# Column sums of a 268 MB matrix on one core: half-precision casting loads and matmuls replaced by float32 loads, a fold on VectorE and matmuls in four column groups

## The chip, the cores and the metric

The kernel runs on one core of a Trainium2 chip. The metric is device time in microseconds (us), from the runs of the kernel; the median of three runs stands for it. A profile of one execution shows when each engine worked; its times count from the start of the span, which goes from the first to the last instruction.

## The reference

The input is float32, 32 x 1024 x 2048. It is summed over its first two axes, so that 32,768 rows become one row of 2,048 sums:

```python
def reference(grad_output):            # (32, 1024, 2048), float32
    return np.sum(grad_output, axis=(0, 1)).astype(np.float32)   # (2048,)
```

Every byte of the input, 268.44 MB, has to be read from HBM once; the output has 8 KB.

## The kernel before

The rows are cut into blocks of 128 rows, one row per partition (1 MB of float32). A plan, made in Python ahead of the instructions, lists the loads in order. Each entry has its first row, the number m of rows per partition, the type in SBUF, the issuing engine and the columns.

- Two entries with m = 1 stay float32 and are issued by the sync engine (SP), as the first loads of the kernel.
- Thirty entries with m = 8 (8 MB in HBM, each partition reading 64 KB in one piece) are issued by GpSimd (POOL), whose DMA queue casts float32 to float16 on the way, so that half the bytes arrive in SBUF. A smaller leftover entry, with m = 2, and a taper of m = 4 and m = 2 follow, then five with m = 1, and the last 128 rows come as four loads of 512 columns each.
- An entry with m > 1 is halved by one VectorE addition in float16 (L152), into a tile `c`. Three buffers are kept for the big `t` tiles and three for `c`.
- TensorE sums over the partitions: a matmul (L161) with a column of ones as the weights turns 128 x 512 values into 1 x 512, added up in PSUM. There are four such accumulators, `psum0` to `psum3`, one for each 512 columns, and each is a single row. In half precision a tile with m = 8 costs 16 matmuls.
- At the end ScalarE and VectorE copy the four accumulators to `res` in turn (L175, L177), and SP sends the 8 KB out (L178).

The tile framework puts in the waits. Each engine works through its instructions in the order of the program, and each of the engines that issue loads does so too. A load into a reused buffer waits until the readers of its old contents are done. The loads themselves share the core's 16 DMA engines.

Of the kernel before, what the change touches and what calls it, by code (L numbers as in the profile page):

```python
# [1 line left out]

# [4 lines left out]

P = 128
MM_N = 512  # L10

PRE_TILES = 2
PRE_M = 1
PRE_ENGS = ("sync", "sync")
BULK_M = 8
BULK_TAPER = (4, 2)
USE_DVE = True
TAIL_TILES = 5
COL_SPLIT_LAST = True
T_BUFS = 3  # L20
C_BUFS = 3
TAIL_BUFS = 8
BULK_ENGS = ("gpsimd",)
OUT_COPY_ENGS = ("scalar", "vector")


@with_exitstack
def kernel(
    ctx: ExitStack,
    tc: tile.TileContext,  # L30
    grad_output: bass.AP,
    out: bass.AP,
):
    nc = tc.nc
    fp32 = mybir.dt.float32
    fp16 = mybir.dt.float16

    D = out.shape[-1]
    flat = grad_output.rearrange("b s d -> (b s) d")
    R = flat.shape[0]  # L40
    assert R % P == 0 and D % MM_N == 0
    nbanks = D // MM_N
    n_row_blocks = R // P

    pre_tiles = min(PRE_TILES, n_row_blocks // PRE_M // 4)
    col_split = COL_SPLIT_LAST and nbanks > 1
    taper = [m for m in BULK_TAPER if m < BULK_M]
    n_small = TAIL_TILES + (1 if col_split else 0)
    while pre_tiles * PRE_M + sum(taper) + n_small > n_row_blocks:
        if TAIL_TILES and n_small > 1:  # L50
            n_small -= 1
        elif taper:
            taper = taper[1:]
        else:
            col_split = False
            n_small = min(n_small, 1)
            break
    n_tail = n_small - (1 if col_split else 0)

    plan: list = []  # L60
    row = 0
    for i in range(pre_tiles):
        plan.append((row, PRE_M, fp32, PRE_ENGS[i % len(PRE_ENGS)], 0, D))
        row += P * PRE_M
    tail_start = R - P * (n_small + sum(taper))
    bi = 0
    while row < tail_start:
        take = min(P * BULK_M, tail_start - row)
        plan.append((row, take // P, fp16, BULK_ENGS[bi % len(BULK_ENGS)], 0, D))
        bi += 1  # L70
        row += take
    for m in taper:
        plan.append((row, m, fp16, BULK_ENGS[bi % len(BULK_ENGS)], 0, D))
        bi += 1
        row += P * m
    for _ in range(n_tail):
        plan.append((row, 1, fp16, BULK_ENGS[bi % len(BULK_ENGS)], 0, D))
        bi += 1
        row += P
    if col_split:  # L80
        for b in range(nbanks - 1, -1, -1):
            plan.append((row, 1, fp16, BULK_ENGS[bi % len(BULK_ENGS)], b * MM_N, MM_N))
            bi += 1
        row += P
    assert row == R

    io_pool = ctx.enter_context(tc.tile_pool(name="io", bufs=T_BUFS))
    pre_pool = None
    if pre_tiles:
        pre_pool = ctx.enter_context(tc.tile_pool(name="pre", bufs=pre_tiles))  # L90
    c_pool = None
    if USE_DVE:
        c_pool = ctx.enter_context(tc.tile_pool(name="csum", bufs=C_BUFS))
    n_small_tiles = n_tail + (nbanks if col_split else 0)
    tail_pool = None
    if n_small_tiles:
        tail_pool = ctx.enter_context(
            tc.tile_pool(name="tail", bufs=min(n_small_tiles, TAIL_BUFS))
        )
    const_pool = ctx.enter_context(tc.tile_pool(name="const", bufs=1))  # L100
    psum_pool = ctx.enter_context(tc.tile_pool(name="psum", bufs=1, space=bass.MemoryType.PSUM))

    ones16 = const_pool.tile([P, 1], fp16)
    nc.vector.memset(ones16[:], 1.0)  # L104
    ones32 = None
    if pre_tiles:
        ones32 = const_pool.tile([P, 1], fp32)
        nc.vector.memset(ones32[:], 1.0)  # L108

    accs = [  # L110
        psum_pool.tile([1, MM_N], fp32, tag=f"psum{b}", name=f"psum{b}")
        for b in range(nbanks)
    ]
    res = const_pool.tile([1, D], fp32)

    def uses_dve(entry) -> bool:
        _, m, dt_, _, _, col_n = entry
        return USE_DVE and dt_ is fp16 and m > 1 and col_n == D

    def n_chunks(entry) -> int:  # L120
        _, m, dt_, _, _, col_n = entry
        n = (m * col_n) // MM_N
        return n // 2 if uses_dve(entry) else n

    total_mm = [0] * nbanks
    for e in plan:
        for j in range(n_chunks(e)):
            total_mm[((e[4] + j * MM_N) % D) // MM_N] += 1
    started = [False] * nbanks
    n_mm = [0] * nbanks  # L130

    for i, entry in enumerate(plan):
        row0, m, dt_, eng_name, col_lo, col_n = entry
        rows = flat[row0 : row0 + m * P]
        if col_n == D:
            src = rows.rearrange("(p m) d -> p (m d)", p=P)
        else:
            src = rows[:, col_lo : col_lo + col_n]

        if dt_ is fp16:  # L140
            big = m > 1 and col_n == D
            pool, tag = (io_pool, "T") if big else (tail_pool, "Ttail")
            T = pool.tile([P, m * col_n], fp16, tag=tag, name=f"t{i}")
        else:
            T = pre_pool.tile([P, m * col_n], fp32, tag="Tpre", name=f"t{i}")
        getattr(nc, eng_name).dma_start(out=T[:], in_=src)  # L146

        red = T
        if uses_dve(entry):
            half = (m * col_n) // 2  # L150
            C = c_pool.tile([P, half], fp16, tag="C", name=f"c{i}")
            nc.vector.tensor_tensor(  # L152
                out=C[:], in0=T[:, :half], in1=T[:, half:], op=mybir.AluOpType.add
            )
            red = C

        w = ones16 if dt_ is fp16 else ones32
        for j in range(n_chunks(entry)):
            b = ((col_lo + j * MM_N) % D) // MM_N
            n_mm[b] += 1  # L160
            nc.tensor.matmul(  # L161
                accs[b][:, :],
                lhsT=w[:],
                rhs=red[:, j * MM_N : (j + 1) * MM_N],
                start=(not started[b]),
                stop=(n_mm[b] == total_mm[b]),
            )
            started[b] = True

    bank_order = list(range(nbanks - 1, -1, -1)) if col_split else list(range(nbanks))  # L170
    for k, b in enumerate(bank_order):
        eng = OUT_COPY_ENGS[k % len(OUT_COPY_ENGS)]
        dst = res[:, b * MM_N : (b + 1) * MM_N]
        if eng == "scalar":
            nc.scalar.copy(out=dst, in_=accs[b][:, :])  # L175
        else:
            nc.vector.tensor_copy(out=dst, in_=accs[b][:, :])  # L177
    nc.sync.dma_start(out=out[None, :], in_=res[:])  # L178


# [1 line left out]
_INS = ['grad_output']  # L182
_OUTS = [((2048,), 'float32')]


# [23 lines left out]
```

## Time and profile before

| what | value |
|---|---|
| three runs, median (lowest to highest) | 628.81 us (628.43 to 628.89) |
| span of the profiled execution, the only time that the page has of it | 627.2 us |
| HBM read over the span | 268.44 MB, 428 GB/s |
| share of 16 DMA engines, GpSimd's casting queue | 98.9% |
| busy: TensorE matmuls / VectorE / GpSimd | 31% / 22% / 4% |
| mean granted TensorE clock | 0.650 of full speed |

The page counts the bytes that were written to SBUF (135 MB for the most part in float16), so its GB/s of DMA is about half of what was read from HBM. The median of the runs is 1.6 us over the profiled span; what lies outside the span is not seen in the profile.

### The profile page before, as it was taken

The page shows a single profiled execution, that of the slowest core. Times are in us where ns is not written, and L with a number is a line of the kernel's source. Part 1 is how long each engine was busy: PE and PEld are TensorE (multiplying, and loading weights), DVE is VectorE, ACT ScalarE, POOL GpSimd, SP SyncE. Part 2 cuts the span into 40 slices and gives each one's busy share as a digit, 9 for nine tenths or more (in the row PEclk, how much of TensorE's full clock was granted, in tenths as well). Part 3 has the DMA queues.
Part 4 walks back from the last instruction along what each step waited for, and adds up shares of the span by engine and source line. Part 5 has one row for each costly group of instructions (what it writes and reads, how often), then busy time and mean ns, then how long its engine had stood idle before and what let it go on. Part 6 is the DMA issues. An engine that isn't in the chain of part 4 may idle for free.

```text
span 627.2 us, 1267 instructions
## 1 busy us (share of the span) xinstructions
PE 195.1 (31%) x536; PEld 58.1 (9%) x536; DVE 138.9 (22%) x37; ACT 2.4 (0%) x3; POOL 22.6 (4%) x46
## 2 busy tenths in 40 slices
PE   3323320333203333123341134321333312343165
PEld 0001100011000111001110011100111000111011
DVE  0202222022220122211222202222022221122320
ACT  0000000000000000000000000000000000000000
POOL 1000000000000000000000000000000000000110
PEclk9677556775567665667655776656676567665677
DMA  9999999999999999999999999999999999999997
GB/s 242 226 234 201 234 201 234 202 232 203 232 203 232 203 232 203 232 204 230 205 230 205 230 205 230 205 230 206 228 207 228 207 224 211 224 211 221 206 206 139
DMA packets 6344, 135.36 MB, mean 216 GB/s; under 512 B 705, under 2 KB 1217, under 8 KB 1857
## 3 DMA queue, kind: packets, MB, share of 16 engines
q0 software_dynamic: 6048, 133.17, 98.9%
q1 hardware_dynamic: 290, 2.11, 0.9%
q8 instruction: 4, 0.07, 0.0%
q14 instruction: 2, 0.02, 0.0%
HBM read 268.44 MB, written 0.01 MB: 428 GB/s over the span
## 4 chain that ended last, share of the span: by engine, by line
another core or an unknown queue 66%; DVE 21%; DMA 11%; PE 1%; POOL 1%; issue 0%; DVEq 0%; POOLq 0%
DVE c L152 20%; DMA t<-in_grad_output_dram 11%; PE psum L161 1%; POOL t L146 1%; DVEq L152 0%; DVE res L177 0%; POOLq L193 0%
## 5 line engine op out<-in xcount | busy, mean ns | idle before, releaser
L161 PE MATMUL psum<-c,ones 128*1 128x512 f16 x496 | 175.9, 533 | 405.5 <-DVE c L152 405.5
L152 DVE TENSOR_TENSOR c<-t 128x8192 f16<-128x8192 f16 (+2 forms) x33 | 137.5, 4167 | 471.1 <-DMA t<-in_grad_output_dram 471.1
L161 PEld LDWEIGHTS <-ones 128*1 128x1 f16 x520 | 56.5, 109 | 537.5 <-issue 516.4
L146 POOL DMA_DIRECT2D t<-in_grad_output_dram x42 | 22.4, 538 | 590.4 <-DVE c L152 575.3
L161 PE MATMUL psum<-t,ones 128*1 128x512 f16 (+1 forms) x40 | 19.4, 639 | 23.5 <-DMA t<-in_grad_output_dram 23.5
L177 DVE COPY res<-psum 1x512 f32<-1x512 f32 x2 | 1.4, 679 | 13.9 <-PE psum L161 13.9
L161 PEld LDWEIGHTS psum<-t,ones 128*1 128x1 f32 x16 | 1.6, 106 | 27.5 <-DMA t<-in_grad_output_dram 14.1
L175 ACT COPY res<-psum 1x512 f32<-1x512 f32 x2 | 1.1, 575 | 621.1 <-PE psum L161 621.1
L175 ACT ACT_TABLE_LOAD x1 | 1.3, 1283 | 0.7 <-PEq L193 0.7
L104 DVE MEMSET ones<- 128x1 f16 x1 | 0.1, 59 | 0.8 <-PEq L193 0.8
L193 POOL MEMSET const-float32-0.0<- 128x1 f32 x1 | 0.1, 100 | 0.2 <-issue 0.2
L193 POOL MEMSET const-bfloat16-1.0<- 128x1 bf16 x1 | 0.1, 103 | 0.0
L193 POOL MEMSET const-float32-1.0<- 128x1 f32 x1 | 0.1, 100 | 0.0
L193 POOL MEMSET const-uint8-127<- 128x1 uint8 x1 | 0.1, 100 | 0.0
L108 DVE MEMSET ones<- 128x1 f32 x1 | 0.1, 59 | 0.0
## 6 DMA issues: line engine op xcount, KB each, us to landing
t<-in_grad_output_dram POOLq DMA_DIRECT2D x30, 4096.0 KB, 53.1
t<-in_grad_output_dram POOLq DMA_DIRECT2D x5, 512.0 KB, 20.4
t<-in_grad_output_dram SPq DMA_DIRECT2D x2, 1024.0 KB, 14.3
t<-in_grad_output_dram POOLq DMA_DIRECT2D x2, 1024.0 KB, 26.6
t<-in_grad_output_dram POOLq DMA_DIRECT2D x1, 2048.0 KB, 29.0
t<-in_grad_output_dram POOLq DMA_DIRECT2D x4, 128.0 KB, 16.1
out_dram<-res SPq DMA_DIRECT2D x1, 8.0 KB
```

The costliest lines, as they stand in the source:

```text
L104: nc.vector.memset(ones16[:], 1.0)
L108: nc.vector.memset(ones32[:], 1.0)
L146: getattr(nc, eng_name).dma_start(out=T[:], in_=src)
L152: nc.vector.tensor_tensor(out=C[:], in0=T[:, :half], in1=T[:, half:], op=mybir.AluOpType.add)
L161: nc.tensor.matmul(accs[b][:, :], lhsT=w[:], rhs=red[:, j * MM_N : (j + 1) * MM_N], start=(not started[b]), stop=(n_mm[b] == total_mm[b]),)
L175: nc.scalar.copy(out=dst, in_=accs[b][:, :])
L177: nc.vector.tensor_copy(out=dst, in_=accs[b][:, :])
L193: nc = _bacc.Bacc("TRN2", target_bir_lowering=False, num_devices=1)
```

## The change

All loads become float32, issued by SP. There are 32 tiles of 1,024 rows. The first 31 are loaded whole (8 MB, 64 KB in each partition) into one of three buffers; in place, three VectorE additions fold the eight rows in each partition to four, two and one; then TensorE sums that one row over the partitions. The last tile's eight rows per partition are not folded: 128 rows each are loaded by themselves, the last of them in two pieces (1,536 and 512 columns), and each goes straight to TensorE.

The sums are laid out anew. The 2,048 columns are cut into a left part of 1,536 and a right part of 512, and each part into four groups, of 384 and of 128 columns. Group g has weights of 32 columns of ones at the array's columns 32g to 32g + 31, and writes PSUM partitions 32g to 32g + 31, all 32 of them the same sum. One row of a tile so takes four matmuls of 384 columns into `accl` and four of 128 columns into `accr`. At the end ScalarE copies `accl` and issues the store of the left part, VectorE copies `accr` and SP issues the store of the right.

```diff
-PRE_TILES = 2
-BULK_M = 8
-BULK_TAPER = (4, 2)
-TAIL_TILES = 5
-BULK_ENGS = ("gpsimd",)
+ROWS = 8
+RING = 3
+GROUPS = 4
+RIGHT = 512
...
-        getattr(nc, eng_name).dma_start(out=T[:], in_=src)
-            nc.vector.tensor_tensor(
-                out=C[:], in0=T[:, :half], in1=T[:, half:], op=mybir.AluOpType.add
-            )
-            nc.tensor.matmul(
-                accs[b][:, :],
-                lhsT=w[:],
-                rhs=red[:, j * MM_N : (j + 1) * MM_N],
...
+    def add_left(row):
+        seen["l"] += 1
+        for g in range(GROUPS):
+            nc.tensor.matmul(
+                accl[g * G : (g + 1) * G, :lw],
+                lhsT=ones[:],                       # 128 x 32, float32
+                rhs=row[:, g * lw : (g + 1) * lw],  # lw = 384
+                start=seen["l"] == 1,
+                stop=seen["l"] == n_rows,
+                tile_position=(0, g * G),
+            )
+
+    def add_right(row):                             # the same, accr, rw = 128
...
+    for i in range(n_tiles - 1):
+        T = io.tile([P, ROWS * D], fp32, tag="T", name=f"t{i}")
+        src = flat[i * P * ROWS : (i + 1) * P * ROWS].rearrange(
+            "(p m) d -> p (m d)", p=P
+        )
+        nc.sync.dma_start(out=T[:], in_=src)
+        m = ROWS // 2
+        while m >= 1:
+            nc.vector.tensor_tensor(
+                out=T[:, : m * D],
+                in0=T[:, : m * D],
+                in1=T[:, m * D : 2 * m * D],
+                op=mybir.AluOpType.add,
+            )
+            m //= 2
+        add_left(T[:, :D])
+        add_right(T[:, :D])
+
+    T = io.tile([P, ROWS * D], fp32, tag="T", name="tail")
+    base = (n_tiles - 1) * P * ROWS
+    for r in range(ROWS):
+        src = flat[base + r * P : base + (r + 1) * P]
+        row = T[:, r * D : (r + 1) * D]
+        if r < ROWS - 1:
+            nc.sync.dma_start(out=row, in_=src)
+        else:
+            nc.sync.dma_start(out=row[:, :left], in_=src[:, :left])
+            nc.sync.dma_start(out=row[:, left:], in_=src[:, left:])
+        add_left(row)
+        add_right(row)
+
+    nc.scalar.copy(out=resl[:], in_=accl[:, :lw])
+    nc.scalar.dma_start(
+        out=out[:left].rearrange("(g w) -> g w", g=GROUPS), in_=resl[::G, :]
+    )
+    nc.vector.tensor_copy(out=resr[:], in_=accr[:, :rw])
+    nc.sync.dma_start(
+        out=out[left:].rearrange("(g w) -> g w", g=GROUPS), in_=resr[::G, :]
+    )
```

The instructions stand on each engine in the order of this text: on TensorE the matmuls of the 31st tile (number 30) come ahead of those of the last eight rows, and on SP the loads come in the order of the rows.

More of the change, by code (lines that the diff above doesn't have):

```diff
@@ L5 @@
 import concourse.tile as tile
-from concourse import bass_utils, mybir
+from concourse import mybir
 from concourse._compat import with_exitstack
 P = 128
-MM_N = 512
-PRE_TILES = 2
-PRE_M = 1
-PRE_ENGS = ("sync", "sync")
-BULK_M = 8
-BULK_TAPER = (4, 2)
-USE_DVE = True
-TAIL_TILES = 5
[L19 to L22, printed above, removed]
-BULK_ENGS = ("gpsimd",)
-OUT_COPY_ENGS = ("scalar", "vector")
+ROWS = 8
+RING = 3
+GROUPS = 4
+RIGHT = 512
 @with_exitstack
@@ L35 @@
     fp32 = mybir.dt.float32
-    fp16 = mybir.dt.float16
     D = out.shape[-1]
@@ L40 @@
     R = flat.shape[0]
[L41 to L53, printed above, removed]
-        else:
-            col_split = False
-            n_small = min(n_small, 1)
-            break
@@ L58 @@
[L58 to L98, printed above, removed]
-        )
-    const_pool = ctx.enter_context(tc.tile_pool(name="const", bufs=1))
-    psum_pool = ctx.enter_context(tc.tile_pool(name="psum", bufs=1, space=bass.MemoryType.PSUM))
@@ L103 @@
[L103 to L145, printed above, removed]
-        getattr(nc, eng_name).dma_start(out=T[:], in_=src)
[L148 to L152, printed above, removed]
-                out=C[:], in0=T[:, :half], in1=T[:, half:], op=mybir.AluOpType.add
[L154 to L161, printed above, removed]
-                accs[b][:, :],
-                lhsT=w[:],
-                rhs=red[:, j * MM_N : (j + 1) * MM_N],
[L165 to L178, printed above, removed]
+    assert R % (P * ROWS) == 0
+    n_tiles = R // (P * ROWS)
@@ new lines @@
+    left = D - RIGHT
+    lw, rw = left // GROUPS, RIGHT // GROUPS
+    G = P // GROUPS
+    io = ctx.enter_context(tc.tile_pool(name="io", bufs=RING))
+    const = ctx.enter_context(tc.tile_pool(name="const", bufs=1))
+    psum = ctx.enter_context(
+        tc.tile_pool(name="psum", bufs=1, space=bass.MemoryType.PSUM)
+    )
+    ones = const.tile([P, G], fp32)
+    nc.vector.memset(ones[:], 1.0)
+    accl = psum.tile([P, 512], fp32, tag="accl", name="accl")
+    accr = psum.tile([P, 512], fp32, tag="accr", name="accr")
@@ new lines @@
+    resl = const.tile([P, lw], fp32)
+    resr = const.tile([P, rw], fp32)
+    n_rows = (n_tiles - 1) + ROWS
+    seen = {"l": 0, "r": 0}
+    def add_left(row):
[9 more added lines that the diff above has]
+            )
@@ new lines, in add_right @@
+    def add_right(row):
+        seen["r"] += 1
+        for g in range(GROUPS):
+            nc.tensor.matmul(
+                accr[g * G : (g + 1) * G, :rw],
+                lhsT=ones[:],
+                rhs=row[:, left + g * rw : left + (g + 1) * rw],
+                start=seen["r"] == 1,
+                stop=seen["r"] == n_rows,
+                tile_position=(0, g * G),
+            )
[16 more added lines that the diff above has]
+        add_right(T[:, :D])
@@ L182 @@
+    nc.scalar.dma_start(
+        out=out[:left].rearrange("(g w) -> g w", g=GROUPS), in_=resl[::G, :]
+    )
+    nc.vector.tensor_copy(out=resr[:], in_=accr[:, :rw])
+    nc.sync.dma_start(
+        out=out[left:].rearrange("(g w) -> g w", g=GROUPS), in_=resr[::G, :]
+    )
 _INS = ['grad_output']
```

## The prediction

> **What bounds the kernel now.** I first read the page's table of DMA queues, its third part (queue, kind: packets, MB, share of 16 engines).
>
> ```profile
> q0 software_dynamic: 6048, 133.17, 98.9%
> q1 hardware_dynamic: 290, 2.11, 0.9%
> ...
> HBM read 268.44 MB, written 0.01 MB: 428 GB/s over the span
> ```
>
> The DMA engines are never idle: the kernel is bound by its loads. The chain of waits (start, length, what) gives their beat and what follows the last one.
>
> ```profile
> 569.53 4.42 DVE c L152
> 573.95 14.81 another core or an unknown queue
> 588.79 0.05 DVEq L152
> 588.85 0.04 issue
> 588.89 4.43 DVE c L152
> ...
> 596.21 24.26 DMA t<-in_grad_output_dram
> ...
> 620.52 3.59 PE psum L161 x8
> 624.10 0.02 issue
> 624.13 0.68 DVE res L177
> ```
>
> An 8 MB tile lands every 19.3 us (588.89 - 569.53 = 19.36; the packets' records repeat at 19.32), which is 434 GB/s read. VectorE then needs only 4.4 us of those 19.3. After the last matmul the span has 627.2 - 624.1 = 3.1 us left, 0.68 of them a copy. So the change can win little in the stream, and its stages behind the last landings decide. Their prices come from the groups of instructions, with shapes kept apart (instructions | busy us, mean ns of one):
>
> ```profile
> L152 DVE TENSOR_TENSOR c<-t 128x8192 f16<-128x8192 f16 x30 | 132.8, 4425 | 459.7 <-DMA t<-in_grad_output_dram 459.7
> L161 PE MATMUL psum<-t,ones 128*1 128x512 f32 x16 | 11.1, 859 | 18.9 <-DMA t<-in_grad_output_dram 18.9
> L152 DVE TENSOR_TENSOR c<-t 128x2048 f16<-128x2048 f16 x2 | 2.5, 1226 | 3.0 <-DMA t<-in_grad_output_dram 3.0
> L152 DVE TENSOR_TENSOR c<-t 128x4096 f16<-128x4096 f16 x1 | 2.3, 2293 | 8.5 <-DMA t<-in_grad_output_dram 8.5
> L177 DVE COPY res<-psum 1x512 f32<-1x512 f32 x2 | 1.4, 679 | 13.9 <-PE psum L161 13.9
> ```
>
> Note the float32 matmuls: two float32 rows of four chunks make eight matmuls in the code and 16 records, so one float32 matmul is two passes. The timeline of weight loads (one ahead of each pass) shows their beat:
>
> ```profile
> 25.86 0.13 PEld L161 LDWEIGHTS psum<-t,ones 128*1 128x1 f32 x1 [0.72 <-issue]
> 26.71 0.13 PEld L161 LDWEIGHTS psum<-t,ones 128*1 128x1 f32 x1 [0.72 <-issue]
> ...
> 28.59 0.08 PEld L161 LDWEIGHTS psum<-t,ones 128*1 128x1 f32 x1 [0.34 <-issue]
> 29.02 0.08 PEld L161 LDWEIGHTS psum<-t,ones 128*1 128x1 f32 x1 [0.34 <-issue]
> ```
>
> A 512-column pass takes 0.855 us after an idle stretch and 0.43 us some 3 to 4 us later. The first float32 row (from 5.74 us on) stayed slow over its whole 6.1 us.
>
> **The stream.** The loads move from GpSimd's casting queue to SP's, reading the same bytes in the same 64 KB pieces and writing twice as many. The packets' records show the cast packet of 64 KB repeating on an engine at 2,413 ns, and SP's float32 packet of 8 KB at 306 ns. Taken as fixed cost plus bytes, (2,413 - 306) / 7 = 301 ns for each 8 KB and 5 ns fixed, one line fits both: float32 writes are no slower there than the cast. A 64 KB float32 packet then takes 2,413 ns, at most 8 x 306 = 2,448. I take the former, since 64 KB pieces are what will be moved; the latter adds 35 ns x 8 packets x 31 tiles = 8.7 us. Beginning at 1.8 us as the loads do now, with 0.9 us for the first packet's latency (the second packets started 1.0 us after the first), 31 tiles end at 2.7 + 31 x 19.32 = 601.6, say 601.5. The last eight rows take 8 x 8 x 0.306 = 19.6 us, the split of the last adds 0.1: the last byte lands at 621.2. Today's last packets end near 622.8 by their records: the cast packets of one row (8 KB read) have 324 ns each, against 306 from SP, and one tile came 0.9 us late. So this edit gains 1 to 2 us at the landing.
>
> **Reuse of the buffers.** A load into one of three buffers waits until the tile three before it is folded and summed, about 15.6 + 3.4 us after its landing, and it is wanted 2 x 19.3 = 38.6 us after it: 19 us of cover. If TensorE took 6.8 us there would still be 16. SP has only these loads queued behind the wait. The tail's first rows wait likewise for tile 28, and the last row's pieces for landings of tile 30 and the first tail row, both well before their turn. I cost them at nothing; without cover each microsecond past 38.6 would be an idle microsecond of the stream, for each tile.
>
> **The fold.** The additions work on 8,192, 4,096 and 2,048 elements in float32, which the trace doesn't show. From below: the half-precision rows, 4.43 + 2.29 + 1.23 = 7.95 us. From above: the float32 copy's 679 ns for 512 elements taken whole, 1.33 ns an element, 19.0 us for 14,336. Of the half-precision rows, (4,425 - 1,226) / 6,144 = 0.52 ns an element, with 160 ns fixed. The copy without those 160 ns is 1.01 ns an element, nearly twice that. I take twice the slope and the fixed part thrice: 14.9 + 0.5 = 15.4 us, 15.6 with the handovers. It hides under 19.3 us of transfer in 30 tiles. In the last folded tile it covers itself no more: TensorE works in order, the matmuls of tile 30 stand ahead of the tail's, so the tail's rows, of which six have landed by then, wait until 601.5 + 15.6 = 617.1.
>
> **TensorE.** From there nine rows are queued: the folded one and the tail's eight. One row is 2,048 columns in two passes each; by the 0.855 us per 512 columns it is 4 x 2 x 0.855 = 6.84 us slow and 3.42 us fast if nothing overlaps (matmul after matmul, as now). With four column groups fully side by side it is a quarter, 1.71 and 0.86. No overlap of column groups is in the trace. I take half: passes start in order, and a group's second pass has to wait for its first, so that only the second pass of one group and the first of the next run together: 3.42 us slow, 1.71 fast. TensorE has been idle for over 10 us, so the first 4.0 us are slow: 4.0 / 3.42 = 1.17 rows, then 7.83 x 1.71 = 13.4 us, together 17.4. The rows all have landed by 621.2 and hide nothing of it. If it never left the slow pace, 9 x 3.42 = 30.8 us.
>
> [...]
>
> **End.** The left copy and store begin ahead of the last 128-column passes. The right copy is 160 + 128 x 1.01 = 0.29 us in place of 0.68, so 3.1 becomes 2.7 us.
>
> **Sum.** 617.1 + 17.4 + 2.7 = 637.2 us of span against 627.2. With the 1.6 us that the runs' median lies over the span, 638.8 us, 1.6% slower.
>
> **Rivals.**
>
> *Four groups side by side.* 4.0 / 1.71 = 2.34 rows, then 6.66 x 0.86 = 5.7, together 9.7: 617.1 + 9.7 + 2.7 + 1.6 = 631.1 us. For it: separate groups with separate outputs. Against: 32 short instructions a row, and two passes of one group.
>
> *No overlap.* 4.0 / 6.84 = 0.58 rows, 8.42 x 3.42 = 28.8, together 32.8: 654.2 us. All matmuls of the trace follow one another like this, but all use the same columns.
>
> *A slower float32 stream.* A view of DMA alone, from 3.2 to 5.2 us, with SP's packets only:
>
> ```profile
> DMA packets 117, 0.84 MB, mean 422 GB/s; under 512 B 14, under 2 KB 14, under 8 KB 14
> ```
>
> At 422 GB/s the 268.44 MB take 636.1 us instead of some 618: +18, so about 656 with the forecast's tail; the 8.7 us above gives 647.5. Against it: the 8 KB packets' fixed part explains the difference. [...] The trace's 8 KB packets already move faster (16 x 8,192 B / 306 ns = 428 GB/s).
>
> *Faster: the backlog never forms.* Place: the fold of tile 30. If VectorE folds float32 at the half-precision rate, 8.2 us with handovers, tail rows are summed from 609.7 on; with four groups side by side TensorE catches up before the last landing, ends 0.9 us after it, and the time is 621.2 + 0.9 + 2.7 + 1.6 = 626.4 us, 0.4% faster. It decides from a fold of 13.2 us downward (614.8 + 9.7 = 624.5, which with 2.7 is the span now). With pairs only it gives 631.4. For it: nothing shows a float32 addition. Against: the copy's 1.01 ns an element.
>
> That the change doesn't do what it says I exclude: the loads, additions and column groups are fixed by the code.
>
> **Chances.** Forecast 0.43, four side by side 0.22, no overlap 0.17, slower stream 0.08, backlog gone 0.06, a stream quicker than the cast's 0.01, a fold near the point of decision 0.03. A measurement of this kernel can tell about 0.2% (1.3 us; its runs lie within 0.5 us). So faster 0.07, same 0.03, slower 0.90. The range, 630 to 655, reaches from four side by side to no overlap and takes in the slow pace throughout (652.2) and the 8.7 us; left out are the gains, the slowest stream, and sums of two mishaps.
>
> **What would show it.** Landings every 19.3 us and DMA full to about 621; three additions of 8.7, 4.4 and 2.3 us; TensorE idle until about 617 and then busy without a gap for some 17 us while nothing lands after 621; passes overlapping in pairs. The forecast is wrong if the additions are done by 610, if the landing beat is not 19.3, or if TensorE's last stretch is near 10 or 33 us.

## The result and the profile after

The changed kernel takes 635.81 us (635.16 to 636.37, 4 runs) against 628.71 us before (4 runs): a ratio of 1.0113, with a 95% interval of 1.0099 to 1.0128. It is 7.1 us slower. The profiled execution took 635.85 us and has a span of 634.1 us.

The DMA queues, in the page's third part, show the same picture as before, with twice the bytes written and the same bytes read:

```profile
q1 hardware_dynamic: 5768, 268.44, 98.1%
...
HBM read 268.44 MB, written 0.01 MB: 423 GB/s over the span
```

The chain of waits (start, length, what) ends with the fold of the last folded tile and TensorE's work behind it; no later landing stands in it:

```profile
564.01 40.43 DMA t<-in_grad_output_dram
604.54 8.70 DVE t L81
613.26 4.44 DVE t L81
617.72 2.30 DVE t L81
620.07 1.51 PE accl L52 x8
```

By the packets' records tile 30 landed at 604.0 us and the last byte of all at 623.9. The timeline from 620 us on shows what TensorE and the stores did (start, length, engine, line, what; x8 is four groups of two passes):

```profile
620.07 1.51 PE L52 MATMUL accl<-t,ones 128*32 128x384 f32 x8 [17.41 <-DVE t L81]
621.35 0.65 PE L64 MATMUL accr<-t,ones 128*32 128x128 f32 x8
...
621.77 1.51 PE L52 MATMUL accl<-tail,ones 128*32 128x384 f32 x8
...
625.88 0.82 PE L52 MATMUL accl<-tail,ones 128*32 128x384 f32 x8
...
629.33 0.82 PE L52 MATMUL accl<-tail,ones 128*32 128x384 f32 x8
...
629.97 0.39 PE L64 MATMUL accr<-tail,ones 128*32 128x128 f32 x8
...
630.22 0.48 ACT L105 COPY resl<-accl 128x384 f32<-128x384 f32 x1 [628.21 <-PE accl L52]
630.44 0.29 DVE L109 COPY resr<-accr 128x128 f32<-128x128 f32 x1 [10.43 <-PE accr L64]
630.73 1.07 ACTq L106 DMA_DIRECT2D out_dram<-resl  x1
630.76 0.65 SPq L110 DMA_DIRECT2D out_dram<-resr  x1
```

Of the matmuls only the first names a wait, for the fold (L81). All later ones follow without a gap, 10.3 us in all, and in the last 6.5 us of them nothing lands any more. The groups of instructions price the fold (instructions | busy us, mean ns of one | idle before):

```profile
L81 DVE TENSOR_TENSOR t<-t 128x8192 f32<-128x8192 f32 x31 | 269.5, 8692 | 139.3 <-DMA t<-in_grad_output_dram 139.3
L81 DVE TENSOR_TENSOR t<-t 128x4096 f32<-128x4096 f32 x31 | 137.2, 4425 | 1.1
L81 DVE TENSOR_TENSOR t<-t 128x2048 f32<-128x2048 f32 x31 | 71.1, 2292 | 1.1
```

### The profile page after: what moved, and what is told of

Read it like the earlier page. It is cut to its first block, busy times and chain, and to the rows that moved or that the text cites. A ratio compares the mean times of both kernels' runs of the same rounds, so it can differ in the third digit from the quotient of the medians.

```text
span 634.1 us, 1523 instructions
## 1 busy us (share of the span) xinstructions
PE 68.3 (11%) x624; PEld 22.7 (4%) x624; DVE 478.1 (75%) x95; ACT 1.8 (0%) x2; POOL 0.2 (0%) x4
## 4 chain that ended last, share of the span: by engine, by line
DMA 67%; DVE 27%; PE 5%; issue 0%; DVEq 0%
DMA t<-in_grad_output_dram 67%; DVE t L81 27%; PE accl L52 4%; PE accr L64 1%; DVE resr L109 0%; DVEq L81 0%
## 5 line engine op out<-in xcount | busy, mean ns | idle before, releaser
L81 DVE TENSOR_TENSOR t<-t 128x8192 f32<-128x8192 f32 (+2 forms) x93 | 477.7, 5136 | 141.4 <-DMA t<-in_grad_output_dram 139.3
L52 PE MATMUL accl<-t,ones 128*32 128x384 f32 x248 | 46.7, 847 | 562.0 <-DVE t L81 562.0
L52 PEld LDWEIGHTS accl<-t,ones 128*32 128x32 f32 x248 | 6.2, 140 | 575.7 <-DVE t L81 575.7
L64 PE MATMUL accr<-t,ones 128*32 128x128 f32 x248 | 20.3, 421 | 0.0
L64 PEld LDWEIGHTS accr<-t,ones 128*32 128x32 f32 x248 | 12.2, 177 | 27.5 <-issue 27.5
L52 PE MATMUL accl<-tail,ones 128*32 128x384 f32 x64 | 7.9, 575 | 0.0
L64 PE MATMUL accr<-tail,ones 128*32 128x128 f32 x64 | 3.4, 293 | 0.0
L64 PEld LDWEIGHTS accr<-tail,ones 128*32 128x32 f32 x64 | 2.2, 124 | 4.2 <-issue 4.2
L52 PEld LDWEIGHTS accl<-tail,ones 128*32 128x32 f32 x64 | 2.2, 127 | 0.1
## 6 DMA issues: line engine op xcount, KB each, us to landing
tail<-in_grad_output_dram SPq DMA_DIRECT2D x1, 256.0 KB, 17.4
```

The source lines that it names most:

```text
L52: nc.tensor.matmul(accl[g * G : (g + 1) * G, :lw], lhsT=ones[:], rhs=row[:, g * lw : (g + 1) * lw], start=seen["l"] == 1, stop=seen["l"] = ...
L64: nc.tensor.matmul(accr[g * G : (g + 1) * G, :rw], lhsT=ones[:], rhs=row[:, left + g * rw : left + (g + 1) * rw], start=seen["r"] == 1, st ...
L81: nc.vector.tensor_tensor(out=T[:, : m * D], in0=T[:, : m * D], in1=T[:, m * D : 2 * m * D], op=mybir.AluOpType.add,)
```

## The experiments

Theory: the time was lost in the backlog on TensorE, which formed since the tail's rows stand behind a fold of 15.5 us. Rival: the float32 stream on SP is late in itself. All runs below were timed beside the kernel before, whose median was 628.9 to 629.1 us there.

**The last folded tile's matmuls moved behind the sixth tail row.** Nothing else is changed.

```diff
-        add_left(T[:, :D])
-        add_right(T[:, :D])
+        if i < n_tiles - 2:
+            add_left(T[:, :D])
+            add_right(T[:, :D])
+        else:
+            last_folded = T
...
         add_left(row)
         add_right(row)
+        if r == ROWS - 3:
+            add_left(last_folded[:, :D])
+            add_right(last_folded[:, :D])
```

> Only the place of the last folded tile's matmuls changes: they stand behind the sixth of the last eight rows instead of ahead of the first. Backlog theory (the changed kernel is late because nine rows wait on TensorE behind the fold of tile 30, which ends at 620.1 us): rows are summed as they land, the last lands at about 623.9 + 0.4, TensorE ends 1.3 to 1.7 us after it, at 625.3 to 625.8 us instead of 630.4, and the time is about 4.5 to 5 us lower, 631. Stream theory (the float32 loads themselves are what is late, and TensorE would end late anyway): no change, 635.8.

Measured: 630.56 us, ratio to the kernel before 1.0029 (1.0018 to 1.0041). That is 5.25 us less than the changed kernel, by the order of instructions alone. TensorE's timeline at the end:

```profile
619.56 0.85 PE L52 MATMUL accl<-tail,ones 128*32 128x384 f32 x8 [0.78 <-DMA tail<-in_grad_output_dram]
...
620.45 0.83 PE L52 MATMUL accl<-t,ones 128*32 128x384 f32 x8
...
622.04 0.85 PE L52 MATMUL accl<-tail,ones 128*32 128x384 f32 x8 [0.55 <-DMA tail<-in_grad_output_dram]
...
623.90 0.85 PE L52 MATMUL accl<-tail,ones 128*32 128x384 f32 x8 [0.79 <-DMA tail<-in_grad_output_dram]
...
624.57 0.40 PE L64 MATMUL accr<-tail,ones 128*32 128x128 f32 x8
```

Each tail row now waits for its own landing, and TensorE ends at 625.0 instead of 630.4. The last byte lands at 624.06, 0.2 us later than in the changed kernel, so the gain is not an earlier landing. The backlog theory holds. The 1.5 us that still lie over the kernel before are in the two spans: the last matmul ends 0.9 us later (624.97 against 624.10) and the stretch behind it is 0.6 us longer (3.7 against 3.1).

**All matmuls in one column group.** The same eight matmuls a row, each group with its own PSUM bank, all in the array's first 32 columns.

```diff
-                accl[g * G : (g + 1) * G, :lw],
+                accl[g][:G, :lw],
...
-                tile_position=(0, g * G),
+                tile_position=(0, 0),
```

> The same matmuls, all in the array's first 32 columns, each group with a PSUM bank of its own; the copies at the end are 4 + 4 of one partition. Four-side-by-side theory: it is the column groups that let nine rows take 10.3 us; without them a row takes 6.84 us slow and 3.42 us fast, nine rows about 33 us, TensorE ends near 653 us and the time is about 23 to 25 us longer, 659 to 661. Rival (the 10.3 us come from cheaper passes of 32 weights, whatever their column): about the same 10.3 us, time near 637.

Measured: 657.85 us, ratio 1.0463 (1.0444 to 1.0482). TensorE's timeline in its last rows:

```profile
639.22 2.74 PE L52 MATMUL accl<-tail,ones 128*32 128x384 f32 x8
641.80 1.04 PE L64 MATMUL accr<-tail,ones 128*32 128x128 f32 x8
642.67 2.74 PE L52 MATMUL accl<-tail,ones 128*32 128x384 f32 x8
```

A row repeats every 3.45 us (642.67 - 639.22), at the full pace. In the changed kernel the rows at full pace repeat every 0.863 us (629.33 - 625.88 = 3.45 for four rows). The column groups so make float32 matmuls 4.0 times as fast; without them nine rows take 33.0 us, as "no overlap" had it. The time is about 1 us under the expected 659 to 661; the stretch behind the last matmul is 3.0 us here against 3.7.

**The fold left out.** This leaves seven eighths of the rows of 31 tiles unsummed.

```diff
-        m = ROWS // 2
+        m = 0
         while m >= 1:
```

> The three additions are left out (so seven eighths of the rows of the first 31 tiles are not summed); loads and matmuls are those of the changed kernel. Backlog theory: TensorE takes tile 30's row at its landing (604.5 us) and is idle when the last row lands, so it ends at about 625.5 us and the time is 5 us lower, near 631, as with late matmuls. If VectorE's traffic in SBUF slows the loads, the beat of 19.35 us falls to 19.32 and the last landing comes about 1 us earlier, time near 630; if not, the beat stays.

Measured: 630.91 us, ratio 1.0035 (1.0023 to 1.0048): 4.9 us less than the changed kernel, about as much as by moving the matmuls. TensorE took tile 30's row at 604.55 us and ended at 625.4. The beat stayed at 19.35 us and the last byte at 624.0. VectorE, busy 75% of the span or not at all, leaves the loads alone.

**The loads cast as before.** Tiles and their weights in half precision, the tail rows and the tiles loaded by GpSimd.

```diff
-    ones = const.tile([P, G], fp32)
+    ones = const.tile([P, G], fp16)
...
-        T = io.tile([P, ROWS * D], fp32, tag="T", name=f"t{i}")
+        T = io.tile([P, ROWS * D], fp16, tag="T", name=f"t{i}")
...
-        nc.sync.dma_start(out=T[:], in_=src)
+        nc.gpsimd.dma_start(out=T[:], in_=src)
```

> Tiles, weights and additions of the changed kernel in half precision, loads cast by the GpSimd queue as before (the rounding of the sums is coarser). Backlog theory: the fold takes 4.4 + 2.3 + 1.2 = 8.0 us instead of 15.4, one pass per matmul makes a row 0.43 us slow, so TensorE has caught up before the last landing and ends within about 1 us of it; with landings at 622 to 624 us the time is 628 to 630. Stream theory (the SP queue's float32 loads land 2 to 3 us late against the casting ones): the last landing moves back to about 621.5 to 622.8, where the backlog theory alone leaves it near 623.9.

Measured: 629.25 us, ratio 1.0007 (0.9998 to 1.0016). VectorE's and TensorE's timelines:

```profile
604.34 8.01 DVE L82 TENSOR_TENSOR t<-t 128x8192 f16<-128x8192 f16 x3 [11.32 <-DMA t<-in_grad_output_dram]
```

```profile
621.49 0.51 PE L53 MATMUL accl<-tail,ones 128*32 128x384 f16 x4 [1.84 <-DMA tail<-in_grad_output_dram]
...
624.02 0.30 PE L65 MATMUL accr<-tail,ones 128*32 128x128 f16 x4 [0.17 <-DMA tail<-in_grad_output_dram]
```

With float32 undone the rest of the change, ring, threefold fold, column groups and single tail rows, costs nothing that can be measured. The last fold still starts at 604.3 us (604.5 with SP's float32 loads), and the last byte lands at 623.67 (623.90 there), so the stream did not move to the 621.5 to 622.8 of the stream theory, which falls. What float32 did is double the fold (15.5 against 8.0 us) and the matmul passes (x8 against x4 for a row's left part).

**Every row to TensorE.** The fold is replaced by eight rows of matmuls a tile.

```diff
-        add_left(T[:, :D])
-        add_right(T[:, :D])
+        for r in range(ROWS):
+            add_left(T[:, r * D : (r + 1) * D])
+            add_right(T[:, r * D : (r + 1) * D])
```

> The fold is left out and every row goes to TensorE: eight rows of a tile take 8 x 0.87 to 8 x 1.71 us, at most 14 of the 19.35 us of a beat. Backlog theory: tile 30's eight rows are done by about 604.5 + 10 = 614.5, TensorE catches up with the tail by 620 and ends 1 to 1.5 us after the last landing; the time is that of late matmuls, 630.5 to 631, apart from instruction loads. Code-load theory: 8,192 TensorE records bring some 30 loads of 16 KB; if each delayed the tile that it meets by 1 us the time would grow by up to 25 us; if only the first matters, since they fall on different DMA engines, by about 1 us.

Measured: 635.49 us, ratio 1.0103 (1.0088 to 1.0119), a miss. Without VectorE TensorE had caught up by the last row as expected, but that row came late: tile 30 landed at 608.76 us, 4.8 us later than in the changed kernel. The page's table of DMA queues has 32 loads of instructions, where the changed kernel has 5:

```profile
q8 instruction: 32, 0.52, 0.3%
```

Over a steady beat of 19.35 us, the 30 beats between the first and the last folded tile's landing are 1.2 us too long in the changed kernel and 6.0 us here. The instruction loads are the difference that I can name, but how they would delay the stream so much is not shown. By the packets' records of the changed kernel each of the 4 instruction loads that fell among its 64 KB packets took 1.01 to 1.07 us, and the packet that started at its end took 2.90 to 2.97 us instead of 2.42: some 1.5 us for each. An estimate from these numbers, 32 x 1.5 us spread evenly over 16 engines, gives 3.0 us, half of the 6.0.

**A running sum on VectorE, the right columns last.** The last folded tile's matmuls stand behind the sixth tail row, as in the first run. VectorE adds up the folded rows of the earlier tiles, so only ten rows go to TensorE in all; of the last two rows the left columns are loaded ahead of the right.

```diff
+        if 0 < i < n_tiles - 2:
+            nc.vector.tensor_tensor(
+                out=run[:], in0=run[:], in1=T[:, :D], op=mybir.AluOpType.add
+            )
...
+    for r in (ROWS - 2, ROWS - 1):
+        nc.sync.dma_start(out=rows[r][:, :left], in_=srcs[r][:, :left])
+    for r in (ROWS - 2, ROWS - 1):
+        nc.sync.dma_start(out=rows[r][:, left:], in_=srcs[r][:, left:])
```

> Late matmuls for the last folded tile as in the run that moved them, and two more edits: VectorE keeps a running sum of the folded rows of tiles 0 to 29 (one more addition of 2,048, 2.3 us a tile, 17.7 of 19.35), so that TensorE has ten rows in all; and of the last two rows the left columns are loaded and summed first, the right ones last, so that the left store is out of the way. Code-load theory (the one beat of 20.5 to 20.7 us goes with the first 16 KB load of instructions during the stream): with some 190 TensorE matmuls and weight loads for each pass kind in place of 624 the loads of instructions are fewer or gone and the last landing is near 622.8 instead of 624.0; rival (the long beat is the input's own): it stays at 624.0. Store theory (the 3.7 us behind the last matmul are ScalarE's store, 1.07 us in issue): with the left store early they fall to about 2.7. Both: time 628 to 628.5, at or just under the kernel before; neither: 630.5.

Measured: 630.22 us, ratio 1.0024 (1.0015 to 1.0033). Tile 30 landed at 603.3, 0.7 us earlier; the one instruction load left fell into the tail (619.9 us) and the last byte landed at 623.9 all the same. The left store was not out of the way: its sums ended at 624.2, and both stores were issued within 0.4 us of each other, with 1.07 and 0.66 us as before. So this run doesn't test the store theory.

**One store, no instruction loads.** The late matmuls and the running sum are kept; the last row comes in 1,536 and 512 columns again. New are four groups of 512 columns, one copy and one store.

```diff
-    nc.scalar.copy(out=resl[:], in_=accl[:, :lw])
-    nc.scalar.dma_start(...)
-    nc.vector.tensor_copy(out=resr[:], in_=accr[:, :rw])
-    nc.sync.dma_start(...)
+    nc.vector.tensor_copy(out=res[:], in_=acc[:, :w])
+    nc.sync.dma_start(out=out.rearrange("(g w) -> g w", g=GROUPS), in_=res[::G, :])
```

> Late matmuls and running sum, with four groups of 512 columns instead of 4 x 384 and 4 x 128 (half as many TensorE instructions: some 160 in all), the last row in pieces of 1,536 and 512 columns, one copy of 512 columns on VectorE (0.68 us) and one store of 8 KB from SP. Store theory (two stores issued at the same time take 1.07 and 0.66 us to issue, one alone 0.32): the stretch from the last matmul to the end of the span is 3.1 us instead of 3.4 to 3.7. Rival (the stretch is the store's own latency, whatever else is issued): 0.4 us longer copy, so about 4.0. Code-load theory: no 16 KB load of instructions meets the stream, every beat is 19.35, the last byte lands at about 622.7 instead of 624.0; rival: a long beat remains, 624.0. With both the time is 628 to 629, with neither 630.5.

Measured: 630.27 us, ratio 1.0020 (1.0011 to 1.0029). Two theories fall. With no instruction load in the stream the 30 beats are still 0.8 us too long, now in three beats of 19.6 to 19.8; so a handful of such loads is not the whole cause. And the store alone takes as long to issue as beside another; the stretch behind the last matmul is 3.5 us, between the 3.1 and the 4.0 of the two theories:

```profile
625.27 0.69 DVE L98 COPY res<-acc 128x512 f32<-128x512 f32 x1 [5.50 <-PE acc L51]
625.99 0.65 SPq L99 DMA_DIRECT2D out_dram<-res  x1
```

SP's store from one partition took 0.32 us to issue before the change and 0.33 in the run with one column group, ScalarE's 0.49 there; from four partitions they take 0.65 and 1.07. It goes with the four partitions (four pieces of the output), not with the number of stores.

**A mixed version.** As the last, with the first tile float32 from SP and all others cast by GpSimd, folded in half precision and added to a float32 running sum; the last folded tile's matmuls stand behind the third tail row.

```diff
+        if i == 0:
+            T = first.tile([P, ROWS * D], fp32, tag="T0", name="first")
+        else:
+            T = io.tile([P, ROWS * D], fp16, tag="T", name=f"t{i}")
...
+        (nc.sync if i == 0 else nc.gpsimd).dma_start(out=T[:], in_=src)
```

> The same, with only the first tile loaded as float32 from SP and all others cast to half precision by GpSimd's queue, folded in half precision and added to the float32 running sum (8.0 + 2.3 us a tile); the last folded tile's matmuls stand behind the third of the last eight rows. Backlog theory: nothing waits on the fold, TensorE ends within 1 us of the last landing. The first load starts as early as in the changed kernel (1.8 us), later ones have the cast's 19.32 us beat: last landing near 622, then 0.5 + 0.4 for TensorE and 3.1 to the end, 626 of span and 627.5 to 628 of time, under the kernel before. If the landings are no earlier than with casting loads alone (623.8), the time is 629.

Measured: 628.74 us, ratio 0.9999 (0.9990 to 1.0008): the kernel before, no better, and a miss: 627.5 to 628 was expected. The last byte landed at 622.9 instead of 622. TensorE ended at 623.8, 0.3 us earlier than in the kernel before, and the stretch behind it was 3.35 us instead of 3.1.

## Why the prediction's direction held, and where its sum was off

The direction and the mechanism held: the stream stayed, and the tail's rows piled up behind the fold of tile 30. The forecast was 10.0 us of loss and 7.1 were measured. That it came so near is luck in part: nine rows took 7.1 us less than put, while the stream was 3.0 us and the end 1.0 us later. And by a sign that the prediction set itself, a last stretch of TensorE near 10 us, its working was wrong there: the first rival's step is what happened. Term by term:

| term | forecast | measured |
|---|---|---|
| start of the last fold | 601.5 | 604.5 |
| fold with handovers, to TensorE's start | 15.6 (617.1) | 15.5 (620.07) |
| nine rows on TensorE | 17.4 | 10.3 |
| from the last matmul to the end of the span | 2.7 | 3.7 |
| span | 637.2 | 634.1 |

**The term that failed is "I take half".** Nine rows were put at 17.4 us and took 10.3; the first rival, four groups side by side, had 9.7. The step assumed that a group's two passes follow one another in the order of issue. The records of the passes show otherwise: for tile 30 four passes start at 620.069, 620.075, 620.082 and 620.089 us, and four more 0.64 us later. The records don't name the group; but in the run with one column group the passes start one by one, 0.32 us apart, so I read the first four as the four groups' first passes. All four groups run at once. The run with one column group measures the factor at 4.0. It is the order of the passes that I had wrong. No run shows the pairs behind the 1.71 us that a fast row was put at; the changed kernel shows all four groups at once and 0.863 us a row.

The slow pace lasted 4.7 us (620.07 to 624.8), against the 4.0 taken. The trace before gave no single value for it. Its first float32 row was slow for 5.1 us (5.74 to 10.81) and not, as the working has it, over its whole 6.1: the last two of its eight passes come 0.44 us apart. Its second row was slow for 2.8 us (25.05 to 27.9).

**The stream was 3.0 us late at the fold.** The beat was 19.35 us instead of 19.32: 0.03 x 30 = 0.9 us (the 64 KB float32 packet took 2,420 ns in the median). One beat of 20.65 added 1.3 us. The kernel before has one too (20.27); the working mentions it in the landings of before and leaves it out of the sum for after. The first tile was 0.3 us later than put, and VectorE started 0.55 us after the last packet's end. So the landing did not gain the 1 to 2 us that the working put: the last byte came at 623.9, 1.1 us later than in the kernel before (622.8). At 8.39 MB / 19.35 us = 434 GB/s the slower-stream rival is out.

**The end was 1.0 us longer.** The right copy took the 0.29 us forecast. But SP's store takes 0.65 us to issue where the working carried over the 0.32 of a store from one partition, and its last packet lands 0.93 us after that (632.34), against 0.74 before. From this landing to the end of the span it takes 1.73 us, against 1.20 in the kernel before (625.96 to 627.16). So half of the 1.0 us lies behind all stores; what fills it is not shown.

**The fold** was priced to 0.1 us: twice the half-precision slope, 8.69 + 4.42 + 2.29, is what the additions took. The faster rival needed a fold under 13.2 us; casting loads, which bring it to 8.0 and halve the passes too, show that the backlog then indeed never forms, and so does the run without a fold. **The reuse of buffers** cost nothing, as put: even at 4.9 to 6.6 us of TensorE a tile, in the run with one group, the beat was 19.35.

## What to carry to other kernels

When a stream bounds a kernel, read what is queued behind the last transfers, engine by engine in the order of issue: work that hides under every beat but the last is paid in full there. Here one fold of 15.5 us ahead of the tail's rows on an in-order engine cost 5.25 us, and issuing the ready rows first took it back without changing any work. Before pricing overlapped matmuls, look at the order of their passes.

## What the hardware showed beyond this

- Float32 matmuls in four column groups ran 4.0 times as fast as in one (0.863 against 3.45 us for 2,048 columns), the passes of the groups side by side.
- The views give the changed kernel a granted clock of 1.0 throughout, while the same 384-column passes came every 0.64 us at 620 us and every 0.32 us at 626. The trace explains it: its clock records begin only at 624.8 us, with the full clock, and the views put 1.0 where there is no record. Where records cover a slow stretch, they show it: in the kernel before the clock is 0.50 from 14.2 to 27.9 us, where 512-column float32 passes come every 0.85 us (26.71 - 25.86), and 1.00 from 27.9 to 38.1 us, where they come every 0.43 us (29.02 - 28.59).
- A store that reads four partitions took about twice as long to issue as one that reads a single partition (0.65 against 0.32 us on SP, 1.07 against 0.49 on ScalarE).
- Over 30 beats the float32 stream of 64 KB packets lost 0.6 to 1.3 us in single long beats, with 4 instruction loads beside it or with none; with 32 it lost 6.0. What the long beats are stays open.
